# Two more weight tiles in the ring, output-stage norms on DVE, a regrouped scatter and a reordered end of the last expert layer

## The chip, the cores and the metric

The kernel runs on one core of a Trainium2 chip. The metric is the device time of one execution in microseconds (us); several executions are taken and their median counts. One profiled execution gives the trace. Engines: PE is TensorE (PEld its weight loads), DVE is VectorE, ACT is ScalarE, POOL is GpSimd, SP is SyncE, which here only issues DMAs.

## What the kernel computes

Two layers over 512 latent tokens of width 1024 and, in layer 0, 256 context tokens that share the weights. Everything is float32.

```python
def layer(x, l):                      # the latent stream; context likewise in layer 0
    sh1, sc1, g1, sh2, sc2, g2 = split(silu(c) @ w_mod[l] + b_mod[l], 6)
    z = (layer_norm(x) * (1 + sc1) + sh1) @ w_in[l]
    y = concat(multiscale_pool(z), spatial_gating(z), attention(z)) @ w_out[l]
    x = layer_norm(ALPHA * x + g1 * y, ln1_g[l], ln1_b[l])
    h = layer_norm(x) * (1 + sc2) + sh2
    aff = softmax(h @ w_router[l])              # 16 experts
    gate, idx = top_k(aff.T, 64)                # each expert takes 64 of the 512 tokens
    hid = silu(h[idx] @ w1) * (h[idx] @ w3)     # w1, w3, w2: 1024 x 1024 for each expert
    m = zeros.at[idx].add((hid @ w2) * gate)
    return layer_norm(ALPHA * x + g2 * m, ln2_g[l], ln2_b[l])
```

## The kernel before

`Net` runs `mixer`, `output` and the experts for each of the two layers. SP's order is written by hand everywhere: each weight tile is loaded when its place in a ring of tiles comes free, in the order of the code. The other engines are ordered by a planner in the first half of the output stage and by hand (the code's order) from the second half on and in the experts.

**Output stage (`output`).** `cats` holds the mixer's result, turned, as a high and a low part; the weights `w_out` are split likewise (`whi`, `wlo`, `ready`), and a product of a 128-token tile with 512 columns is three matmuls for each of eight k (`mm3`). Half 0 is done for all latent tiles, then half 1. In half 1 the tiles move through a pipeline over m, one tile a step: `product`, `residual` (times g1, plus ALPHA times the residual, statistics), `variance`, `norm1` (first normalisation), `gained` and `shifted` (times ln1's gain, plus its bias), `variance2`, `norm2` (second normalisation), `table` (rows stored to HBM for the gathers), `turn` (transposes), `score` (router product) and `logit`. The last latent tile is "urgent" and is worked in halves. GpSimd computes 1/sigma as a power in `rstd`; `shift` makes -m * r for ACT's normalisation. `router` then finds each expert's 64 tokens by eight rounds of max and match on DVE, and `mod_group` and `gates2` make g2 for the experts. In layer 0 two context tiles are worked in the same stage after the latent ones.

**Experts of layer 1 (`experts_last`).** `weight_stream` hands out tiles of 1 MB (four for a 1024 x 1024 matrix) in a fixed round: ring1 3, cat 4, ring2 5, ring 4, ring3 1, 17 in all. cat is the mixer's result, ring2 the output stage's weights, ring3 the place of its remaining buffers; the tiles of ring hold w_mod's groups 10 and 11 until `mod_group` has used them. `fetch` gathers an expert's 64 rows on GpSimd's queue, four experts ahead, into xg; `inputs` turns them and applies scale (DVE) and shift (GpSimd). Expert e is then worked as first (w1), second of e - 1 (w2), third (w3). The results of two experts make a pair: `second` writes them to two half tiles, which are split into `yhi` (ACT) and `ylo` (DVE, GpSimd), and `scatter` adds them to the token rows by a product with one-hot columns (`picks`), 8 products and 8 DVE additions in a pair. Pairs are (0,1) to (14,15). For the last pair, `base` puts the rows into eight PSUM banks by a product with the identity, the pair is added there, and `total` normalises each tile: statistics, ACT normalisation, gain (GpSimd and DVE), bias (DVE), store. `affine` spreads ln2's gain and bias over the partitions, at expert 13.

Layer 0's experts (`experts`, not changed) work both streams with gathers and scatter-adds over HBM.

## Time and profile before

| what | us |
|---|---|
| median of 3 runs | 1815.21 (1815.08 to 1815.95) |
| the profiled execution | 1820.27 |
| its span, first to last instruction | 1818.5 |
| PE busy | 1624.8 (89%) |
| DVE / ACT / POOL busy | 649.1 / 399.5 / 371.8 |
| DMA | 527.19 MB, 290 GB/s in the mean |

In the order of the trace: the mixer of layer 0 until about 320, its output stage until about 430, its experts until about 980, the mixer of layer 1 until about 1215, its output stage and router until 1315, its experts and the end until 1818.5. Matmuls are pipelined, so that a busy PE is not PE at its peak. A row in order of time reads: start in us, duration in us, engine, line of the kernel, operation, output<-input by the tiles' names, partitions x elements, and in brackets the idle time before it with what ended it. One float32 matmul of the code leaves two records, one of the split products one.

### The profile page before, as it was taken

To read this page: it belongs to the slowest core of one execution; us is meant where nothing else is said; L and a number is where in the kernel's file an instruction comes from. 1 tells how busy PE (TensorE), PEld (TensorE's weight loads), DVE (VectorE), ACT (ScalarE), POOL (GpSimd) and SP (SyncE) were. 2 spreads that over 40 slices of the span, in tenths; PEclk is the share of its full clock that TensorE was granted. 3 is DMA by queue.
4 is the path that set the end of the run, shared out by engine and by line. 5 is a ranking of instruction groups with operands and counts; after the bars stand their busy time and mean duration, and the time that the engine had idled before them with its cause. 6 is when DMAs were issued, how large, how long until landed. Compare 5 with 4: busy or idle time off the path is not lost. (4 is left out here: it accounts for less than half of the span.)

```text
span 1818.5 us, 26146 instructions
## 1 busy us (share of the span) xinstructions
PE 1624.8 (89%) x10859; PEld 849.2 (47%) x10859; DVE 649.1 (36%) x1360; ACT 399.5 (22%) x742; POOL 371.8 (20%) x352
## 2 busy tenths in 40 slices
PE   6988997996999999999996888998699988987994
PEld 3766874752444444344432666776233332332231
DVE  4443663683111111111115855666512221222124
ACT  3333664243000000000002534562300000000001
POOL 2422211142212212112112432212101010100003
PEclk9999999997999999999997898999699999999998
DMA  9441029368999999999997271134899999999992
GB/s 330 149 156 47 1 77 339 134 226 324 362 401 397 396 400 398 395 400 392 401 393 241 79 258 56 54 136 173 319 380 408 409 408 409 409 409 409 409 409 99
DMA packets 160606, 527.19 MB, mean 290 GB/s; under 512 B 10548, under 2 KB 13620, under 8 KB 160232
## 3 DMA queue, kind: packets, MB, share of 16 engines
q1 hardware_dynamic: 147172, 489.47, 69.5%
q0 software_dynamic: 10720, 27.46, 5.1%
q10 hardware_dynamic: 2596, 8.59, 1.2%
q8 instruction: 86, 1.41, 0.3%
q14 instruction: 32, 0.26, 0.0%
HBM read 506.61 MB, written 18.87 MB: 289 GB/s over the span
## 5 line engine op out<-in xcount | busy, mean ns | idle before, releaser
L1325 PE MATMUL h<-ring,xT 128*64 128x512 f32 x1448 | 326.3, 599 | 15.4 <-DMA ring<-in_w 11.5
L1325 PEld LDWEIGHTS h<-ring,xT 128*64 128x64 f32 x1448 | 100.0, 137 | 217.4 <-issue 187.8
L1325 PE MATMUL y<-ring,gpart 128*64 128x512 f32 x760 | 172.8, 597 | 8.6 <-DMA ring<-in_w 7.6
L216 PE MATMUL s<-whi,cat 128*128 128x512 f32 x352 | 147.3, 420 | 10.3 <-ACT whi L884 6.1
L217 PE MATMUL s<-wlo,cat 128*128 128x512 f32 x352 | 145.4, 413 | 8.6 <-DVE wlo L212 7.5
L218 PE MATMUL s<-whi,cat 128*128 128x512 f32 x352 | 144.3, 410 | 2.3 <-DVE cat L430 2.3
L1325 PE MATMUL h<-cat,xT 128*64 128x512 f32 x600 | 137.5, 602 | 6.4 <-DMA cat<-in_w 4.3
L1577 POOL DMA_INDIRECT acc<-y,rows x32 | 51.0, 1594 | 396.7 <-DVE y L1576 396.5
L1325 PEld LDWEIGHTS y<-ring,gpart 128*64 128x64 f32 x760 | 51.9, 137 | 119.8 <-issue 108.9
L1344 ACT ACTIVATE hT<-tr 128x64 f32<-128x64 f32 x34 | 7.3, 225 | 423.0 <-DVE hT L1346 421.3
L1405 DVE SCALAR_TENSOR_TENSOR half<-y,gates,g 64x512 f32<-64x512 f32 x32 | 24.0, 750 | 183.3 <-PE y L1325 182.9
L216 PEld LDWEIGHTS s<-whi,cat 128*128 128x128 f32 x352 | 69.2, 198 | 31.7 <-ACT whi L884 8.7
L217 PEld LDWEIGHTS s<-wlo,cat 128*128 128x128 f32 x352 | 69.2, 197 | 29.0 <-DVE wlo L212 10.8
L1325 PEld LDWEIGHTS h<-cat,xT 128*64 128x64 f32 x600 | 41.2, 138 | 88.1 <-issue 75.5
L1344 ACT ACTIVATE gpart<-tr 128x256 f32<-128x256 f32 x32 | 12.3, 384 | 313.3 <-DVE gpart L1346 313.2
L754 DVE TENSOR_REDUCE am<-s 128x1 f32<-128x768 f32 (+1 forms) x68 | 65.9, 970 | 37.1 <-PE s L751 36.9
L218 PEld LDWEIGHTS s<-whi,cat 128*128 128x128 f32 x352 | 69.1, 196 | 18.9 <-DVE cat L430 3.5
L1325 PE MATMUL c<-ring,xT 128*32 128x256 f32 x1344 | 77.6, 380 | 0.0
L751 PE MATMUL s<-kT,qT 128*128 128x256 f32 (+1 forms) x288 | 71.4, 370 | 5.9 <-ACT zq L766 5.5
L766 ACT ACTIVATE zq<-s,anm 128x768 f32<-128x768 f32 (+1 forms) x80 | 65.1, 816 | 27.2 <-DVE anm L756 26.2
L152 PE MATMUL bk<-ring,cc 128*32 128x512 f32 x384 | 53.5, 676 | 19.1 <-DMA ring<-in_w_mod 18.5
L800 PE MATMUL po<-y,Z 128*64 128x128 f32 x832 | 67.1, 285 | 2.1 <-DVE zt L817 2.1
(350 smaller groups left out, 2297.3 us busy)
## 6 DMA issues: line engine op xcount, KB each, us to landing
ring<-in_w SPq DMA_DIRECT2D x276, 1024.0 KB
cat<-in_w SPq DMA_DIRECT2D x108, 1024.0 KB
ring<-in_w_mod SPq DMA_DIRECT2D x48, 1024.0 KB
ring<-in_w_in SPq DMA_DIRECT2D x12, 1024.0 KB
ring<-in_w_out SPq DMA_DIRECT2D x10, 1024.0 KB
tab<-nn ACTq DMA_DIRECT2D x10, 512.0 KB
acc<-res ACTq DMA_DIRECT2D x6, 512.0 KB
fin<-acc SPq DMA_DIRECT2D x6, 512.0 KB
```

The lines of the kernel that those rows point to most:

```text
L152: nc.tensor.matmul(ps[32 * t:32 * t + 32, :], self.sil[:, k, :], wm[k], start=k < 4, stop=k >= 4)
L216: nc.tensor.matmul(ps, ahi, bhi, start=start, stop=False)
L217: nc.tensor.matmul(ps, ahi, blo, start=False, stop=False)
L218: nc.tensor.matmul(ps, alo, bhi, start=False, stop=stop)
L751: nc.tensor.matmul(sp[:, nk * m + b0:nk * m + b1], qT[t][:, 2 * j + h, :], kT[:, 2 * h + x, k0 + b0:k0 + b1], start=x == 0, stop=x == 1)
L754: nc.vector.tensor_reduce(mx, sp[:, :nk * n].rearrange("p (m k) -> p m k", k=nk), axis=AX.X, op=OP.max)
L766: nc.scalar.activation(pbuf[:, i % 3, nk * m:nk * m + nk], sp[:, nk * m:nk * m + nk], AF.Exp, bias=nm[:, m:m + 1], scale=QK_SCALE, accum_o ...
L800: nc.tensor.matmul(po[t][64 * h:64 * h + 64, 128 * j:128 * j + 128], Z0[:, c0 + c, 128 + 64 * h:192 + 64 * h], pT[:, 128 * c:128 * c + 128 ...
L1325: self.nc.tensor.matmul(outs[s][o:o + cap, :], stat[s][:, k, :], w[k][:, n * t:n * t + n], start=k == 0, stop=k == KC - 1)
L1344: nc.scalar.activation(o[:, r], pv[:, r], AF.Copy)
L1405: nc.vector.scalar_tensor_tensor(ys[j][(r + odd) % 2][p], y[p], gates[p, e:e + 1], g2[odd][p], op0=OP.mult, op1=OP.mult)
L1577: nc.gpsimd.indirect_dma_start(out=self.acc[l, s], out_offset=bass.IndirectOffsetOnAxis(ap=rows[:, e:e + 1], axis=0), in_=y, in_offset=Non ...
```

## The change

1. ring3 of layer 1 has 3 tiles for 1. Room for them: the gathers' xg has 1 buffer for 4, `iota` moves into a tile that stood already, the tiles of ln2's rows go into a ring tile that `take` takes out of the round at expert 6.
2. The gathers run one expert ahead. For expert 0 only its own is issued before its inputs, and scale and shift of expert 0 are done in one operation per 128 columns, half on DVE, half on ACT.
3. Output stage, latent tiles, both layers: `norm1` becomes (x - m) * gain on DVE and `variance2` x * r + bias on DVE, by halves; ACT's first normalisation, GpSimd's gain and DVE's addition go. Context tiles stay.
4. Layer 1: g1's second half is multiplied into the second half of `w_out` in `ready`, and `residual` of half 1 reads PSUM without a product.
5. Layer 1: `mod_group` 10 and 11 move from behind the scores into steps LT and LT + 1 of the pipeline; `gates2` stays.
6. `shift` is a tensor_scalar with r as pointer.
7. Pairs become (0), (1,2) to (13,14), (15); `slots` has a ninth column, filled with -1 where no expert stands. `scatter` comes after the third product. `affine` moves to expert 7. Four bases run within the last w1; within and after the last w3 the pair (13,14) is scattered or added to them. `total`: statistics, (x - m) * gain on DVE out of PSUM, then ACT times r and GpSimd plus bias (the very last half by DVE), store.

```diff
-RING2, RING3 = (2, 5), (7, 1)
+RING2, RING3 = (2, 5), (7, 3)
...
-        self.nc.vector.scalar_tensor_tensor(nb, m, -1.0, r, op0=OP.mult, op1=OP.mult)
+        self.nc.vector.tensor_scalar(nb, m, r, -1.0, op0=OP.mult, op1=OP.mult)
...
             for k in ks:
+                if last and half:
+                    nc.vector.tensor_mul(raw[k], raw[k], g1[0][:, 512:])
...
-            self.iota = self.T(keep, [128, S], "iota")
+            self.iota = self.T(self.small, [128, S], "mpart", bufs=1)
...
+            if last and half:
+                tmp = pss[t]
+            else:
+                tmp = self.T(op, [128, 512], "otmp", bufs=2)
+                nc.vector.tensor_mul(tmp, pss[t], g1[where[t][0]][:, hs])
...
+            if t < LT:
+                for c in halves:
+                    nc.vector.scalar_tensor_tensor(res[t][:, c], res[t][:, c], m, lg[:, c],
+                                                   op0=OP.subtract, op1=OP.mult)
+            else:
+                nc.scalar.activation(res[t], res[t], AF.Identity, bias=self.shift(m, r), scale=r)
...
+                if t < LT:
+                    nc.vector.scalar_tensor_tensor(res[t][:, c], res[t][:, c], mom[t][1], lb[:, c],
+                                                   op0=OP.mult, op1=OP.add)
                 nc.vector.bn_stats(st[:, i], res[t][:, c])
...
-                        for g in range(2):
-                            self.mod_group(l, 10 + g, wm[g])
                         gates2()
...
                     stage(score, m - 3)
+                    if m < LT + 2:
+                        self.mod_group(l, 10 + m - LT, wm[m - LT])
...
-            self.slots = self.T(keep, [128, 2, NE // 2], "slots")
+            self.slots = self.T(keep, [128, 2, NE // 2 + 1], "slots")
+            nc.gpsimd.memset(self.slots, -1.0)
...
+        def take():
+            m = count[0] % len(turns)
+            pool, tag, n = turns[m]
+            turns[:] = turns[m + 1:] + turns[:m]
+            count[0] = 0
+            return self.T(getattr(pool, tag) if pool is self else pool, [128, 2048], tag, bufs=n)
...
+            if e == 0:
+                for b in range(4):
+                    nc.vector.tensor_scalar(o[:, 0, b], pv[:, 0, b], sc2[:, b, 0:1], sh2[:, b, 0:1],
+                                            op0=OP.mult, op1=OP.add)
+                    nc.scalar.activation(o[:, 1, b], pv[:, 1, b], AF.Identity, bias=sh2[:, 4 + b, 0:1],
+                                         scale=sc2[:, 4 + b, 0:1])
+                return
...
+            j, odd = (e + 1) // 2, e % 2
             y = self.P("y")
             self.product(weights("w2", e), {0: y}, {0: hT.pop(e)}, None, odd, between)
+            if e in (0, NE - 1):
+                one = self.T(keep, [128, 512], "half", bufs=2)
+                nc.vector.scalar_tensor_tensor(one, y, gates[:, e:e + 1], g2[odd], op0=OP.mult, op1=OP.mult)
+                ys[j] = [parted(one, nc.vector)] * 2
+                return
...
+        def before_last(j):
+            for i in range(3):
+                yield True
+            for i in range(3):
+                scatter(j, 2 + i // 2, i % 2, "tr")
+                yield True
+                if i < 2:
+                    yield True
+            for i in range(4):
+                add(j, *divmod(i, 2), final[divmod(i, 2)], False, False)
+                if i == 1:
+                    scatter(j, 3, 1, "tr")
+            yield True
...
             for h, c in enumerate(halves):
+                nc.vector.scalar_tensor_tensor(acc[t][:, c], final[t, h], m, norm["g"][:, c],
+                                               op0=OP.subtract, op1=OP.mult)
             yield True
+            for h, c in enumerate(halves):
+                if t == LT - 1 and h == 1:
+                    nc.vector.scalar_tensor_tensor(acc[t][:, c], acc[t][:, c], r, norm["b"][:, c],
+                                                   op0=OP.mult, op1=OP.add)
+                else:
+                    nc.scalar.activation(acc[t][:, c], acc[t][:, c], AF.Copy, scale=r)
+                    nc.gpsimd.tensor_add(acc[t][:, c], acc[t][:, c], norm["b"][:, c])
                 nc.sync.dma_start(self.out[128 * t:128 * t + 128, c], acc[t][:, c])
...
+        fetch(0)
         inputs(0)
+        fetch(1)
+        end = NE - 1
+        for e in range(NE):
+            first(e, (lambda: turn(e - 1)) if e else None, [based()] if e == end else ())
+            if e == NE // 2 - 2:
+                own = self.take()
...
+            if e % 2:
+                picks(e // 2)
             if e:
+                second(e - 1, [affine()] if e == NE // 2 else ())
             inputs(e + 1)
+            fetch(e + 2)
+            late = [before_last(e // 2)] if e == end else []
+            third(e, late)
+            step(late, 100)
+            if e % 2 and e < end:
+                for t in range(LT):
+                    for h in range(2):
+                        scatter(e // 2, t, h)
...
+        second(end)
+        base(2, 0, "h")
+        base(2, 1, "h")
+        for x in range(2):
+            for t in range(2):
+                for h in range(2):
+                    add(j, t, h, final[t, h], False, True, (x,))
...
-        self.xg[e, s] = self.T(self.wk, [128, 1024 // REPS[s]], f"xg{s}", bufs=4 if l == DEPTH - 1 else 3)
+        self.xg[e, s] = self.T(self.wk, [128, 1024 // REPS[s]], f"xg{s}", bufs=1 if l == DEPTH - 1 else 3)
```

## Rows read from the trace of the kernel before

**Rows 1.** The table of stretches, five of layer 1: busy us of each engine, clock, DMA.

```profile
1225.00:1240.00 15.00, 15.00 (x66) 12.06 (x65) 8.43 (x15) 3.44 (x6) 0.00 (x0) 1.00 0.22 87
1262.00:1305.00 43.00, 30.30 (x162) 13.88 (x162) 30.55 (x84) 18.97 (x28) 8.78 (x8) 0.72 1.00 370
1305.00:1325.00 20.00, 11.75 (x47) 5.06 (x48) 2.38 (x13) 0.79 (x4) 5.02 (x5) 0.66 0.52 173
1325.00:1722.00 397.00, 351.94 (x1520) 120.80 (x1518) 87.19 (x150) 22.25 (x42) 33.95 (x32) 0.97 1.03 408
1722.00:1779.00 57.00, 51.81 (x206) 16.74 (x206) 11.91 (x20) 4.68 (x9) 2.33 (x2) 1.00 1.02 405
```

**Rows 2.** Waits of PE by releaser, 440 to 960: us, times, longest.

```profile
PE tr L1334 <- DMA xg<-tab,rows: 2.4, 1, 2.4
```

**Rows 3.** DVE in order of time, both layers: start, us, operation, idle before.

```profile
406.93 2.30 DVE L205 SCALAR_TENSOR_TENSOR lnnb<-lnmv,lnr 128x1 f32<-128x1 f32 x1 [0.51 <-POOL lnr L181]
...
973.36 0.95 DVE L440 CAST whi<-ring 128x512 fp32r<-128x512 f32 x1
...
1252.81 0.69 DVE L934 TENSOR_TENSOR otmp<-s,g 128x512 f32<-128x512 f32 x1 [2.19 <-PE s L218]
...
1269.00 2.31 DVE L205 SCALAR_TENSOR_TENSOR lnnb<-lnmv,lnr 128x1 f32<-128x1 f32 x1 [0.72 <-POOL lnr L181]
...
1271.94 0.69 DVE L935 SCALAR_TENSOR_TENSOR res<-res,otmp 128x512 f32<-128x512 f32 x1
...
1283.22 0.16 DVE L205 SCALAR_TENSOR_TENSOR lnnb<-lnmv,lnr 128x1 f32<-128x1 f32 x1 [0.72 <-POOL lnr L181]
...
1300.80 0.21 DVE L1256 CAST half<-ri 32x128 f32<-32x128 uint32 x1
...
1805.87 7.96 DVE L1453 TENSOR_TENSOR res<-res,norm 128x512 f32<-128x512 f32 x6
```

**Rows 4.** GpSimd in order of time, same columns, both layers.

```profile
406.87 2.33 POOL L960 TENSOR_TENSOR res<-res,lb 128x1024 f32<-128x1024 f32 x1
...
972.91 1.11 POOL L1557 TENSOR_TENSOR hid<-hid,y 128x256 f32<-128x256 f32 x1 [1.49 <-ACT y L1556]
...
1251.98 2.39 POOL L956 TENSOR_TENSOR res<-res,lg 128x1024 f32<-128x1024 f32 x1 [1.55 <-ACT res L949]
...
1268.94 2.34 POOL L956 TENSOR_TENSOR res<-res,lg 128x1024 f32<-128x1024 f32 x1
```

**Rows 5.** PE in order of time, router and first products, both layers.

```profile
360.03 1.61 PE L992 MATMUL bk<-ident,nn 128*128 128x128 f32 x8 [2.63 <-ACT nn L979]
...
1290.47 6.21 PE L152 MATMUL bk<-ring,cc 128*32 128x512 f32 x32
...
1305.51 1.51 PE L1262 MATMUL bk<-ident,half 32*128 32x16 f32 x8 [0.82 <-ACT half L1257]
...
1312.73 1.09 PE L1334 MATMUL tr<-ident,xg 128*128 128x128 f32 x4 [5.71 <-DMA xg<-tab,rows]
...
1315.85 4.63 PE L1325 MATMUL h<-ring,xT 128*64 128x512 f32 x12 [2.03 <-POOL xT L1381]
```

**Rows 6.** The gathers' tile xg, whole run: from issue to landing.

```profile
DMA to landing us min/median/max: 3.5/6.4/7.6
```

**Rows 7.** PE in order of time, the last two products of layer 1.

```profile
1770.71 6.23 PE L1325 MATMUL h<-ring,xT 128*64 128x512 f32 x28
...
1786.07 3.60 PE L1325 MATMUL y<-cat,gpart 128*64 128x512 f32 x16
```

**Rows 8.** Waits of PE, 1315 to 1780, the longest in total.

```profile
PE sc L1419 <- ACT yhi L1410: 16.1, 7, 2.3
```

**Rows 9.** Groups by line and shape, 1779 to the end: busy, mean, idle before.

```profile
L1450 POOL TENSOR_TENSOR res<-res,gain 128x512 f32<-128x512 f32 x6 | 9.3, 1582 | 0.0
L1453 DVE TENSOR_TENSOR res<-res,norm 128x512 f32<-128x512 f32 x8 | 9.2, 1214 | 0.0
...
L1441 DVE BATCH_NORM_STATS2 lnst<-sc 128x6 f32<-128x512 f32 x2 | 1.4, 698 | 1.2 <-PE sc L1439 1.2
```

More of the change, by code (lines that the diff above doesn't have):

```diff
@@ L1384, in stat, with first @@
             return {0: xT[e]}
-        def first(e, middle):
+        def first(e, middle, between=()):
             h1 = self.P("h")
-            self.product(weights("w1", e), {0: h1}, stat(e), middle)
+            self.product(weights("w1", e), {0: h1}, stat(e), middle, between=between)
             hid[e] = self.T(self.small, [128, 512], "gpart", bufs=2)
@@ L1406, in second @@
                                                op0=OP.mult, op1=OP.mult)
[L1407 removed]
+            if not odd:
                 for h in range(2):
[L1409 to L1421 removed]
@@ L1423, in experts_last, with add @@
-        final, norm = {}, {}
-        def base(n, *tags):
-            for m, tag in enumerate(tags, n):
-                t, h = divmod(m, 2)
-                final[t, h] = self.P(tag)
-                nc.tensor.matmul(final[t, h], self.ident, acc[t][:, 512 * h:512 * h + 512], start=True, stop=False)
-                yield True
+                    ys[j][h] = parted(ys[j][h], nc.gpsimd if h else nc.vector)
+        def add(j, t, h, pt, start, stop, xs=(0, 1)):
+            for x in xs:
+                nc.tensor.matmul(pt, oh[j, h][:, 128 * t:128 * t + 128], ys[j][h][x],
+                                 start=start and x == 0, stop=stop and x == 1)
@@ new lines, in scatter, with base, based @@
+        def scatter(j, t, h, tag="sc"):
+            pt = self.P(tag)
+            add(j, t, h, pt, True, True)
+            c = slice(512 * h, 512 * h + 512)
+            nc.vector.tensor_add(acc[t][:, c], acc[t][:, c], pt)
+        final, norm = {}, {}
+        def base(t, h, tag):
+            final[t, h] = self.P(tag)
+            nc.tensor.matmul(final[t, h], self.ident, acc[t][:, 512 * h:512 * h + 512], start=True, stop=False)
+        def based():
+            for i, tag in enumerate(("sc", "sc", "bk", "tr")):
+                base(*divmod(i, 2), tag)
+                yield True
@@ L1436, in total @@
             st = self.T(self.small, [128, 2, 6], "lnst", bufs=4)
             for h in range(2):
-                for x in range(2):
-                    nc.tensor.matmul(final[t, h], oh[j, h][:, 128 * t:128 * t + 128], ys[j][h][x],
-                                     start=False, stop=x == 1)
                 nc.vector.bn_stats(st[:, h], final[t, h])
@@ L1457, in affine @@
         def affine():
-            norm["g"], norm["b"] = self.T(wk, [128, D], "gain"), rows_
+            rows_ = norm["b"]
             banks = []
@@ L1475, in turn @@
             hT[e] = self.hidden(0, hid.pop(e), self.T(self.small, [128, 512], "gpart", bufs=2))
-        rows_ = self.T(wk, [128, D], "norm")
         self.xg = {}
-        for e in range(4):
-            fetch(e)
+        fetch(0)
         inputs(0)
-        for e in range(NE + 1):
-            if e < NE:
-                first(e, (lambda: turn(e - 1)) if e else None)
-            else:
-                turn(e - 1)
-            if e == 1:
-                nc.sync.dma_start(rows_[:2], self.a["ln"][l, 2:4])
-            if e and e % 2 == 0:
-                picks(e // 2 - 1)
-            if e:
-                second(e - 1, {NE - 2: [affine()], NE - 1: [base(0, "sc", "sc", "bk")],
-                               NE: [base(4, "tr", "h", "h")]}.get(e, ()))
-            if e == NE:
-                stages = [total(t) for t in range(LT)]
-                for m in range(LT + 3):
-                    if m == 1:
-                        step([base(7, "y")])
-                    for g in stages[max(0, m - 3):m + 1][::-1]:
-                        next(g)
-            elif e and e % 2 == 0:
-                scatter(e // 2 - 1)
-            inputs(e + 1)
-            fetch(e + 4)
-            if e < NE:
-                third(e, [base(3, "tr")] if e == NE - 1 else ())
@@ new lines, in experts_last @@
+        j = NE // 2
+        turn(end)
+        picks(j)
+        second(end)
[5 more added lines that the diff above has]
+                    add(j, t, h, final[t, h], False, True, (x,))
+        stages = [total(t) for t in range(LT)]
+        next(stages[0])
+        for t in range(2, LT):
+            if t == LT - 1:
+                base(t, 0, "tr")
+                base(t, 1, "y")
+            for h in range(2):
+                add(j, t, h, final[t, h], False, True)
@@ L1508, in gather @@
+        for m in range(1, LT + 1):
+            for g in stages[max(0, m - 1):m + 1][::-1]:
+                next(g)
+                if m > 0 and g is stages[m - 1]:
+                    next(g)
     def gather(self, l, e, s, route):
-        self.xg[e, s] = self.T(self.wk, [128, 1024 // REPS[s]], f"xg{s}", bufs=4 if l == DEPTH - 1 else 3)
+        self.xg[e, s] = self.T(self.wk, [128, 1024 // REPS[s]], f"xg{s}", bufs=1 if l == DEPTH - 1 else 3)
         self.nc.gpsimd.indirect_dma_start(
```

49 lines of the change are left out of this document (12 added, 37 removed).

## The prediction

> **What bounds the kernel now.** I read the page's 40 slices first, then the table of stretches, the waits of PE, and the engines in order of time around the change. The table [rows 1] says that in the experts of layer 1 the DMA engines are full (share 1.03 at 408 GB/s, then 1.02) from 1325 us until the last weight has come at about 1779; so the end of that stream is fixed by where DMA was idle before. The reader is to see one hole: between 1305 and 1325 the share is 0.52. Every tile ahead of the products is loaded by then, and the first comes free only when PE has begun. 0.52 where a full stretch reads 1.03 leaves 20 x (1 - 0.52/1.03) = 9.9 us unused. Behind the stream stands a tail without weights: 1818.5 - 1779 = 39.5 us.
>
> In the experts of layer 0 the bound is PE: from 440 to 960 it waited most for one gather, 2.4 us, and for no weights [rows 2]. There an earlier start of the products moves everything behind it.
>
> **Layer 0, output stage.** `norm1`, `gained` and `variance2` of the latent tiles become four scalar_tensor_tensor on DVE instead of an ACT pass, a GpSimd product and a DVE addition. The price of one is that of the residual's, 0.69 us for 128x512 [rows 3]. DVE's own work of a tile is then the residual 3 x 0.69, two of `norm1` 1.38, four operations of 0.69 in `variance2` 2.76, and small ones about 0.8: 7.0 us, in layer 1 6.3, since the residual loses its product there. Before, it was about 6 plus waits. These waits are the gain: at 1269.00 a 128x1 operation took 2.31 us, because GpSimd's product began at 1268.94 and took 2.34 [rows 3, 4]. The DVE product of PSUM with SBUF at 1252.81 lasted its 0.69 beside GpSimd's product of 1251.98, so only operations on SBUF alone waited. `norm1` also needs only the mean, so GpSimd's power for 1/sigma runs beside it. I replay DVE's order with these prices from the first residual of the second half: the first tile's last normalisation starts about 2 us earlier, and this is the 2.63 us that PE stood before the transposes at 360.03 [rows 5]. PE is nearly full after that, so I take 2.5 us for layer 0; bounds 0.5 (PE's own work decides) and 4. As PE waits for no weights there, it goes through to the end.
>
> **The shift.** `shift` turns from two SBUF inputs into a tensor_scalar with one. In layer 0 it stood for 2.30 us at 406.93 in the middle of the top-k, beside GpSimd's 406.87 [rows 3, 4]. Would the new form wait too? The nearest row with one SBUF input is the cast at 973.36, of 0.95 us beside GpSimd's 972.91 to 974.02 [rows 3, 4]: it waited. So I take nothing for it, and 3 us as the upper bound (2.2 there, about 1 where the layers join).
> The Trainium skill (SBUF — State Buffer, section Who interferes with whom) says that a DVE operation with at most one SBUF input contends with GpSimd only in a two-port mode, and that tensor_scalar is one that can enter it. If a single column does not enter it, that rule gives the 3 us; no row here has this form beside GpSimd.
>
> **Layer 1, from the output stage to the first product.** The eight products that gate the second half of the weights cost DVE 8 x 0.69 = 5.5 us, and four residual products of 0.69 go. DVE is busy 8.43 of the 15 us from 1225 [rows 1], ahead of these weights' splits; the 6.6 idle us hide them. Without that cover PE would wait up to 5.5 us at the start of the second half. Replaying as above, the last tile's shift, at 1283.22 before [rows 3], comes near 1279.3. But one modulation group, half of 6.21 us [rows 5], now lies on PE ahead of that tile's transposes; it takes back 2 to 3, so I keep 1.5. Bounds -1 and 4.
> More certain is the next step: top-k ends on DVE at 1301.0 [rows 3], yet PE reaches its product at 1305.51, because the two modulation groups (from 1290.47) and eight gate products of 1 us lie before it in PE's queue [rows 5]. With the groups moved, the gate products start near 1290 and end before top-k does: 4.3 us. The first expert's inputs skip the GpSimd addition and go by DVE and ACT side by side: 1 of the 3.1 us between 1312.73 and 1315.85 [rows 5]. PE begins 6.8 us earlier, near 1309 on the old time axis.
> The groups' moving also frees four ring tiles earlier; that is worth nothing by itself, since DMA was full from 1262 to 1305 [rows 1], and would be 4 us of stream if it were not.
>
> **Two more ring tiles.** They carry 2.1 MB, 5.1 us at 408 GB/s, so the stream fills until about 1312 instead of 1307. The first tile comes free some 3 us after the first product (TensorE is granted 0.66 in that stretch), and DMA came back about 5 us after that product: now near 1314. Of the 9.9 idle us 2 to 3 stay: 7 gained. Bounds 2 (the added tiles lie over the output stage's last buffers and come free late) and 9.9 (no hole). Their room comes from the gathers' four buffers becoming one. A gather lands 3.5 to 7.6 us after its issue [rows 6] and is issued about one expert before its use, 12.6 MB or 31 us of weights, which hides it; uncovered it would cost PE 6.4 an expert. The tile lent to the norm's rows leaves the ring at the seventh expert; the stream is full then, and loses nothing.
>
> **The tail.** Pairs now begin with expert 0 alone and end with 15 alone, so that 13 and 14 are scattered within the last w3, the affine rows are made at expert 7, and four sums are based within the last w1. Reckon from the last landing L. Before, the last y ended at 1789.67 [rows 7], L + 10.7, though only eight of its 32 records need follow L: PE was behind by the affine rows, the wait for y's halves (16.1 us in seven pairs [rows 8]) and the bases. Now: last w3 tile at L - 10.3 (4.2 MB), its records until L - 8.5, a scatter and the sums of 13 and 14 until L - 5.1, gate product, transposes and copy until L - 4, then 32 records of 0.22 us (28 took 6.23 [rows 7]), 7.0: L + 3.
> Then half, hi and lo, three operations of about 0.7, and the first sums: DVE's statistics start at L + 6.5. DVE has four tiles of 2 x 0.70 and small ones 0.36, and eight products with the gain of about 0.72: 12.8, until L + 19.3 (0.70 is the statistics in [rows 9]). ACT scales beside it. GpSimd adds the bias, 1.2 each by half of its 1024-wide product [rows 4]; the last ones follow DVE, L + 22. Before, GpSimd's products and DVE's additions alternated, 1582 and 1214 ns in the mean [rows 9]; DVE's new products read PSUM and need not wait. From DVE's last addition, which ended at 1805.87 + 7.96 = 1813.83 [rows 3], to the end of the span were 4.7 us. So L + 26.7 against L + 39.5 is 12.8; I take 12, for some waits at the end. Bounds 7 (GpSimd and DVE still alternate in the last six adds, and PE is at half clock in the final sums) and 14.
>
> **Sum.** 2.5 + 7 + 12 = 21.5 us. The profiled execution took 1820.27, its span 1818.5; the median of the runs is 1815.21, 5 below it, and I take the sum off that: 1793.7.
>
> **The rivals.**
> Ring without effect: the added tiles come free when the hole is nearly over. For: they share addresses with what the output stage uses last; against: that use ends near 1290 and these tiles are last in the ring's order. Gain there 2 instead of 7: 1798.7. Chance 0.13.
> Shift free of GpSimd: 3 us more, 1790.7. For: one column, one SBUF input; against: the cast. Chance 0.2.
> Half a tail: PE or GpSimd stays behind, 5 there for 12: 1800.7. Chance 0.09.
> Slower: the single gather buffer. Each gather must wait for the transposes of the expert before. PE is busy 351.94 of 397 us [rows 1], 12.9 experts at 31 us, 27.3 each, 437 for 16; from 1309 to the last y near 1775 (old axis) there are 466, so from 1.8 us of stall an expert PE decides. At 3.1 the change comes to nothing; at 4 it costs 16 x 2.2 = 35: 1829. Against it stands the lead of a whole expert over a landing of 7.6. Chance 0.05, and 0.03 for a stall near 3.
>
> **How the numbers follow.** The forecast holds 0.5: 1793.7, with 1787 to 1799 for it alone, as not all terms fail to one side. The range takes in the free shift and the two weaker gains: 1786 to 1802. A change under 0.2% (3.6 us) is what a measurement of this kernel cannot tell from none. Faster is the sum of forecast, ring, shift and tail, 0.92; within 0.2% 0.03; slower 0.05.
>
> **What would show it.** Right: a DMA share above 0.85 in the 20 us around layer 1's first product; the router's last product on PE as soon as top-k ends; the last y within 5 us of the last landing, and 27 us from that landing to the end; layer 0's experts 2 to 3 us earlier. Wrong: PE waiting for gathers in layer 1, the same hole of 9.9 us, GpSimd additions near 1.6 us in the tail.

## The result, and the profile after

The changed kernel takes 1796.3 us (median, 1793.7 to 1802.6) against 1815.1 for the kernel before in the same series: 0.9901 of it, 95% interval 0.9875 to 0.9927. Forecast were 1793.7 (1786 to 1802) and "faster" at 0.92. So 18.8 us were gained where 21.5 were forecast. The profiled execution took 1802.63 us, its span 1800.8.

Executions of one and the same kernel differ by 8 to 9 us within a series of the changed kernel, and by 18 in one series of the kernel before. Much of it lies before layer 1: in eight profiles with the same code until there, the first product of layer 1's mixer starts anywhere from 992 to 1002 us. From that product to the end three profiles of the changed kernel agree within 0.6 us. So I split this stretch at the same marks in every profile (us between marks, starts of the rows named; "first residual" is DVE's first operation on the results of the output stage's second half):

```
                                                  before   changed (3 profiles)     difference
mixer's first product -> first residual           245.97   243.91 243.66 243.94     -2.1
-> last product of the output stage                21.62    17.67  17.68  17.68     -3.9
-> last cast of the top-k on DVE                   31.99    31.67  31.67  31.66     -0.3
-> the router's last product on PE                  4.71     5.74   5.74   5.73     +1.0
-> transposes of the gathered rows                  7.22     9.60   9.55   9.42     +2.3
-> first product of expert 0                        3.12     1.58   1.58   1.58     -1.5
-> end of the last y                              473.82   464.27 464.30 463.88     -9.7
-> end of the span                                 28.83    24.55  24.60  24.56     -4.3
sum                                               817.28   798.99 798.78 798.45    -18.5
```

The kernel before has one profile of its own in this table. Two later series gained 24.7 and 21.8 us by the medians (below, ref and ref2), more than these 18.5; what layer 0 adds is read further down.

The table of stretches of the changed kernel (times, busy us of PE, PEld, DVE, ACT and POOL, granted clock, DMA share, GB/s), for [rows 1]:

```profile
1264.00:1308.00 44.00, 29.75 (x150) 9.49 (x138) 24.59 (x86) 14.51 (x24) 3.69 (x6) 0.68 1.02 412
...
1304.00:1308.00 4.00, 0.00 (x0) 0.00 (x0) 0.48 (x4) 0.00 (x0) 1.08 (x1) 0.50 1.03 410
1308.00:1312.00 4.00, 1.10 (x6) 0.73 (x6) 0.34 (x1) 0.04 (x1) 0.24 (x1) 0.50 0.09 33
1312.00:1316.00 4.00, 4.00 (x10) 1.23 (x12) 1.03 (x3) 2.74 (x5) 0.74 (x1) 0.50 0.24 66
1316.00:1320.00 4.00, 4.00 (x18) 1.28 (x16) 0.00 (x0) 0.12 (x1) 0.00 (x0) 0.84 0.80 262
...
1770.00:1771.00 1.00, 1.00 (x8) 0.35 (x6) 0.00 (x0) 0.00 (x0) 0.00 (x0) 1.00 0.71 279
1771.00:1772.00 1.00, 1.00 (x8) 0.37 (x6) 0.00 (x0) 0.00 (x0) 0.00 (x0) 1.00 0.44 180
```

The hole is still there. From 1308 to 1320 the shares leave 12 - 4 x (0.09 + 0.24 + 0.80)/1.03 = 7.6 us unused, where 2 to 3 were forecast. What is new stands in the first line: 412 GB/s ahead of the hole, where [rows 1] had 370. In 43 us that is 1.8 MB more, nearly the two added tiles; why the rate rose no run shows. The ring was full at 1308, not at 1312. The stream ends at about 1771 in place of 1779 (read where its share falls off, to some 0.3 us).

PE from the output stage to the first product, for [rows 5]:

```profile
1269.60 3.53 PE L152 MATMUL bk<-ring,cc 128*32 128x512 f32 x16
...
1277.23 1.92 PE L152 MATMUL bk<-ring,cc 128*32 128x512 f32 x16 [0.74 <-DVE rl L1025]
...
1284.73 1.97 PE L1053 MATMUL bk<-gpart,selb 128*64 128x512 f32 x2
...
1298.01 1.97 PE L1055 MATMUL bk<-half,selb 1*64 1x512 f32 x2
1300.80 1.89 PE L1266 MATMUL bk<-ident,half 32*128 32x16 f32 x8 [0.82 <-ACT half L1261]
1310.40 1.09 PE L1349 MATMUL tr<-ident,xg 128*128 128x128 f32 x4 [7.72 <-DMA xg<-tab,rows]
1311.98 7.96 PE L1340 MATMUL h<-ring,xT 128*64 128x512 f32 x24 [0.50 <-DVE xT L1395]
```

The two modulation groups fit into PE's pauses. The eight gate products behind them (first and last shown) take 1.97 us each, where the prediction reckoned with 1, and end at 1299.98. In the kernel before (first and last of the eight, then the granted clock there) they took 1.07 at full clock; in the changed kernel (last line) the clock was at half:

```profile
1296.61 1.07 PE L1049 MATMUL bk<-gpart,selb 128*64 128x512 f32 x2
...
1303.62 1.07 PE L1051 MATMUL bk<-half,selb 1*64 1x512 f32 x2
```

```profile
1297.00:1305.00 8.00, 7.68 (x16) 1.32 (x14) 3.87 (x16) 1.23 (x3) 0.00 (x0) 1.00 1.02 405
```

```profile
1284.00:1300.00 16.00, 15.76 (x18) 2.42 (x18) 10.15 (x42) 3.73 (x5) 0.00 (x0) 0.50 1.02 410
```

DVE had ended the top-k long before, at 1295.27 (last row; the rows ahead of it are for the shift, in both layers):

```profile
406.33 0.21 DVE L205 TENSOR_SCALAR lnnb<-lnmv,lnr 128x1 f32<-128x1 f32 x1 [0.53 <-POOL lnr L181]
...
409.89 1.11 DVE L1259 CAST half<-ri 32x128 f32<-32x128 uint32 x1
...
1276.83 0.21 DVE L205 TENSOR_SCALAR lnnb<-lnmv,lnr 128x1 f32<-128x1 f32 x1 [0.72 <-POOL lnr L181]
...
1295.06 0.21 DVE L1260 CAST half<-ri 32x128 f32<-32x128 uint32 x1
```

GpSimd beside it, in both layers:

```profile
406.27 2.35 POOL L965 TENSOR_TENSOR res<-res,lb 128x1024 f32<-128x1024 f32 x1
408.58 2.34 POOL L961 TENSOR_TENSOR res<-res,lg 128x1024 f32<-128x1024 f32 x1
...
1304.80 1.08 POOL L1576 DMA_INDIRECT xg<-tab,rows  x1 [27.94 <-DVE gates L1287]
```

At 406.33 the shift takes 0.21 us in the middle of a GpSimd addition, where the old form stood 2.30 [rows 3]. The first gather is issued at 1304.80, while weights still stream, and its transposes start 5.6 us later. Behind it PE waits for no other gather; its waits from 1312 to 1772 are mostly for weights, of which this is the largest (us in total, times, longest):

```profile
PE h L1340 <- DMA ring<-in_w: 18.7, 29, 1.2
```

The end: PE's last y, the last operation of DVE and of GpSimd, and GpSimd's group with its mean, for [rows 7] and [rows 9]:

```profile
1769.17 3.65 PE L1340 MATMUL y<-cat,gpart 128*64 128x512 f32 x16 [0.52 <-DVE gpart L1361]
1772.65 3.60 PE L1340 MATMUL y<-ring,gpart 128*64 128x512 f32 x16
```

```profile
1791.34 0.75 DVE L1497 SCALAR_TENSOR_TENSOR res<-res,lnr,ring 128x512 f32<-128x512 f32 x1
```

```profile
1790.19 4.24 POOL L1501 TENSOR_TENSOR res<-res,ring 128x512 f32<-128x512 f32 x3
```

```profile
L1501 POOL TENSOR_TENSOR res<-res,ring 128x512 f32<-128x512 f32 x7 | 9.2, 1338 | 0.9 <-ACT res L1500 0.9
```

With L = 1771 the last y ends at L + 5.3, DVE at L + 21, GpSimd at L + 23.4, the span at L + 30.

### The profile page after: what moved, and what is told of

It reads as the page before. It is cut to its first block, busy times and chain, and to the rows that moved or that the text cites. A ratio compares the mean times of both kernels' runs of the same rounds, so it can differ in the third digit from the quotient of the medians.

```text
span 1800.8 us, 26188 instructions
## 1 busy us (share of the span) xinstructions
PE 1621.4 (90%) x10875; PEld 841.3 (47%) x10875; DVE 643.8 (36%) x1378; ACT 390.7 (22%) x735; POOL 348.2 (19%) x344
## 5 line engine op out<-in xcount | busy, mean ns | idle before, releaser
L1340 PE MATMUL h<-ring,xT 128*64 128x512 f32 x1504 | 343.6, 601 | 21.8 <-DMA ring<-in_w 18.7
L1340 PE MATMUL y<-ring,gpart 128*64 128x512 f32 x720 | 162.5, 596 | 9.3 <-DMA ring<-in_w 8.8
L1340 PE MATMUL h<-cat,xT 128*64 128x512 f32 x544 | 125.7, 604 | 9.9 <-DMA cat<-in_w 7.8
L1340 PEld LDWEIGHTS h<-cat,xT 128*64 128x64 f32 x544 | 37.0, 138 | 85.9 <-issue 69.4
L1340 PE MATMUL y<-cat,gpart 128*64 128x512 f32 x304 | 69.7, 597 | 3.5 <-DMA cat<-in_w 3.0
```

Of the source, the lines that this page charges most:

```text
L1340: self.nc.tensor.matmul(outs[s][o:o + cap, :], stat[s][:, k, :], w[k][:, n * t:n * t + n], start=k == 0, stop=k == KC - 1)
```

## The experiments

Each is judged by the marks above, from its profile, with the medians beside them:

```
                mixer's first     of it, from the  to router's   to expert 0's  to the   sum     median (lowest to highest)
                to output's last  first residual   last product  first product  end
before          267.59            21.62            36.70         10.34          502.65   817.28
ref             261.34            17.68            37.41         11.13          488.90   798.78  1793.1 (1791.6 to 1799.6)
ref2            261.62            17.68            37.39         11.00          488.44   798.45  1797.3 (1790.6 to 1799.8)
e_ring          260.93            17.68            37.36          9.29          494.76   802.34  1796.3 (1793.5 to 1801.7)
e_shift         262.37            17.63            37.26         11.18          488.09   798.90  1796.6 (1793.1 to 1800.4)
e_gates1        259.48            17.69            31.11         12.20          489.03   791.82  1792.2 (1787.7 to 1795.2)
e_gates01       261.49            17.68            31.31         12.13          489.67   794.60  1789.5 (1788.5 to 1790.6)
best            261.61            17.69            31.31         12.14          488.94   794.00  1788.5 (1784.8 to 1793.0)
e_mod11         261.54            17.68            37.39         11.00          487.85   797.78  1792.5 (1789.7 to 1797.8)
e_tail          265.95            21.69            33.58          9.30          494.75   803.58  1803.9 (1801.0 to 1812.1)
e_out0          261.52            17.68            37.40         11.15          489.53   799.60  1796.9 (1794.1 to 1798.3)
e_norm1         261.20            17.25            35.22         12.11          489.41   797.94  1793.6 (1790.7 to 1797.5)
e_ungated       261.76            18.41            38.00          9.74          489.57   799.07  1797.2 (1796.1 to 1800.2)
```

Runs were made in three groups, each on one chip: ref, e_gates1, e_ring, e_shift; then e_tail, e_mod11, e_gates01, e_out0; then ref2, best, e_norm1, e_ungated. The kernel before had medians of 1817.7, 1816.9 and 1819.0 there. In the texts put on record before the runs, "the last product of the mixer" is the output stage's last product.

How far the marks can be trusted is read from runs whose edit lies elsewhere. From the first residual to the output stage's last product nine profiles of the same code give 17.67 to 17.69. Ahead of the first residual profiles of the same code differ by 2.2 us (241.8 in e_gates1 to 244.0 in e_norm1), from expert 0's first product to the end by 1.8 (487.9 to 489.7). Differences below that are not resolved there.

**The changed kernel again (ref).**

> The changed kernel again, unedited, as the measure for the three that run with it on this chip. Its runs so far lie between 1793.7 and 1802.6 us, a wider spread than that of the kernel before (1814.7 to 1816.0), so a difference of a term is read against this run and not against the first ones. Expected: 1794 to 1798.

1793.1, 1 us below the expected span; 0.9861 (0.9839 to 0.9884) of the kernel before on this chip. In the third group 1797.3.

**Two ring tiles less (e_ring).**

```diff
-RING2, RING3 = (2, 5), (7, 3)
+RING2, RING3 = (2, 5), (7, 1)
```

> The changed kernel with one tile in the last ring in place of three, nothing else. Theory of the prediction: the two tiles are 2.1 MB, 5.1 us at 408 GB/s, so the stream stops 5.1 us earlier (at about 1303), DMA's hole is as much longer, and the time is 5 us more. First rival: the tiles come free late and carry nothing: 0 to 1 us more. Second rival: with them DMA is full while the gather is under way, and without them the gather lands faster (3.5 us in place of 5.5 in the changed kernel's trace), which gives 2 us back: 3 us more.

From the first product to the end 5.9 us more: the two tiles carry what the prediction gave them (5.1). But the stretch to the first product is 1.8 shorter. Stretch, gather and transposes of this run, from the table of stretches, GpSimd and PE:

```profile
1292.00:1296.00 4.00, 0.43 (x3) 0.33 (x2) 1.63 (x11) 0.00 (x0) 1.08 (x1) 0.50 0.09 34
```

```profile
1294.56 1.08 POOL L1576 DMA_INDIRECT xg<-tab,rows  x1 [27.91 <-DVE gates L1287]
```

```profile
1298.26 1.09 PE L1349 MATMUL tr<-ident,xg 128*128 128x128 f32 x4 [5.82 <-DMA xg<-tab,rows]
```

DMA is idle when the gather is issued, and it is there after 3.7 us, not 5.6. That is the second rival. The tiles are worth 5.9 - 1.8 = 4.1 us net; the sums of the table give 802.34 - 798.7 = 3.6, the medians 3.3.

**The gates (e_gates1, then both layers: e_gates01).** `gates2` takes the numbers of the tiles that it makes; in layer 1:

```diff
-                        gates2()
+                        gates2((0,))
...
                 step([lat], 100)
+                gates2((1,))
```

> Layer 1: only the first of the two gate tiles (four of eight products) is made before the end of the top-k, the second behind the router's last product, in the time in which PE waits for the gather. Theory, the gate products decide: in the changed kernel they hold PE from 1284.73 to 1299.98 at 1.97 us each while top-k ends on DVE at 1295.2; with four of them PE is free at 1292.6 and the router's last product starts at about 1296.1 instead of 1300.80. The other four (7.9 us) end near 1306, when the gather lands. Then the first product is 4.7 us earlier, the idle stretch of DMA shorter by as much, and the time 4 to 5 us less. Rival, the gather among the weights decides: it is issued earlier into full queues and lands no earlier than about 1309, or the four products stand before its transposes; then 0 to 1.5 us.

> The changed kernel with the second gate tile behind the router in both layers. Layer 1 as in the run with that layer alone: the router's last product 31.1 us after the mixer's last product instead of 37.4, and 5 us less to the end. Layer 0, theory that the gate products decide there too: they end at 412.0 in the changed kernel while the top-k ends at about 411; with four of them left behind the router its last product starts about 1.5 us earlier and the experts of layer 0 with it; 6.5 us less than the changed kernel in all. Rival for layer 0: the context tile's transposes, which wait for DVE and ACT, stand before the gather's in PE's queue and decide: 0 from layer 0.

In layer 1 the router's last product came 6.1 to 6.3 us earlier behind the output stage, the first product 5.0 to 5.2 earlier; one more is lost on the gather, which now lands among weights all the time. PE in the run with both layers:

```profile
1282.62 1.97 PE L1057 MATMUL bk<-half,selb 1*64 1x512 f32 x2
1286.90 1.89 PE L1270 MATMUL bk<-ident,half 32*128 32x16 f32 x8 [2.31 <-ACT half L1265]
1288.72 1.97 PE L1055 MATMUL bk<-gpart,selb 128*64 128x512 f32 x2
...
1297.45 1.08 PE L1353 MATMUL tr<-ident,xg 128*128 128x128 f32 x4 [1.08 <-DMA xg<-tab,rows]
```

PE is idle 2.31 us before the router's product: now top-k decides. So the gate products were the bound in the changed kernel, as the theory said. From the first product to the end nothing changes (488.9 to 489.7), so the 5 us of start go through to the end. The medians of the first group show only 0.9 us of it, the repeat below 8.7: a handful of runs does not resolve such a term. Of e_gates1's sum, 1.9 us lie ahead of the output stage's last product, where nothing was edited. In layer 0, from the first residual of the second half to the first expert product, 83.8 in place of 85.5: 1.8 us, but 0.8 of them lie ahead of the gate products. The 1.0 behind the last product is of the size expected; TensorE's clock moves this stretch by more (see e_out0), so for layer 0 the theory is not shown.

**One modulation group back before the gates (e_mod11).**

```diff
+                        self.mod_group(l, 11, wm[1])
                         gates2()
...
-                    if m < LT + 2:
+                    if m < LT + 1:
```

> The changed kernel with the second modulation group back in front of the gate products (the first stays beside the scores). In the kernel before both groups (6.21 us) stood there and the gate products behind them took 1.07 us each; in the changed kernel PE has pauses there and they take 1.97. Theory, what PE did before sets the granted clock: the group takes 3.5 us at half clock from 1284.7 on, the eight gate products about 1.07 each behind it, and the router's last product starts about 4 us earlier: 33.5 us after the last product of the mixer instead of 37.4. Rival, the clock stays at 0.50 behind one group: the group and the products together last 19 us, the router's product comes 3 us later, 40.5.

Neither: 37.39, as without the edit. PE:

```profile
1277.52 3.64 PE L152 MATMUL bk<-ring,cc 128*32 128x512 f32 x16
1281.09 1.97 PE L1053 MATMUL bk<-gpart,selb 128*64 128x512 f32 x2
1282.99 1.08 PE L1055 MATMUL bk<-half,selb 1*64 1x512 f32 x2
...
1287.47 1.96 PE L1055 MATMUL bk<-half,selb 1*64 1x512 f32 x2
```

and its clock:

```profile
1281.00:1283.00 2.00, 2.00 (x7) 0.30 (x3) 1.97 (x9) 0.60 (x1) 0.00 (x0) 0.50 1.02 408
1283.00:1287.00 4.00, 4.00 (x9) 0.75 (x8) 3.90 (x17) 0.60 (x1) 0.00 (x0) 0.93 1.03 410
1287.00:1293.00 6.00, 6.00 (x7) 0.86 (x6) 0.98 (x5) 0.00 (x0) 0.00 (x0) 0.50 1.03 410
```

The clock did rise to full speed behind the group, but it was taken back at 1287 while the gate products went on. Gates and group together take as long as the gates alone at half clock. What kept it up for eight products in the kernel before is left open; both groups back in front were not tried.

**The end alone (e_tail).** The kernel before with `experts_last`, `take`, the slots and the single gather buffer of the changed one.

> The kernel before with only the experts of layer 1 changed (regrouped pairs, bases, affine rows at expert 7, gathers one ahead, first inputs on DVE and ACT, the norms of the end). The ring, the output stage, the shift, the gates and the modulation groups stay as before. Theory: from the last landing to the end 39.2 becomes 29.9 as in the changed kernel, since nothing else in the change touches that stretch; the first product comes 1.5 us earlier; so 9.5 to 11 us less than before in all, and from layer 1's first product to the end 493 us instead of 502.7. Prediction on record: 12 from the last landing. Rival: part of the 9.3 us came from the earlier stream, and the regrouping alone gives 5.

From the first product to the end 494.75 for 502.65: 7.9 us, 1.8 less than the theory's 493 stands for. The rival of 5 is out. The inputs take 1.6 in place of 3.1, as in the changed kernel. In all it is 13.7 us faster by the marks, 13.0 by the medians, more than the 9.5 to 11 expected: 4.8 of it lie before the router's product, where nothing was edited. 1.7 of these come ahead of the first residual, 3.1 behind the output stage, where both modulation groups took 3.64 us for 6.21 (granted clock from 1290 to 1297: 1.00 for 0.59). Whether chance or a side effect, one profile each leaves open; by it, the column of the kernel before may be up to 4.8 us too slow in the first table. In its output stage, which is the old one, DVE and PE show the stall that the change was to remove:

```profile
1259.43 2.31 DVE L205 SCALAR_TENSOR_TENSOR lnnb<-lnmv,lnr 128x1 f32<-128x1 f32 x1 [0.65 <-POOL lnr L181]
```

```profile
1263.07 1.82 PE L992 MATMUL bk<-ident,nn 128*128 128x128 f32 x8 [2.63 <-ACT nn L979]
...
1289.29 3.64 PE L152 MATMUL bk<-ring,cc 128*32 128x512 f32 x32
```

**The old shift (e_shift).**

```diff
-        self.nc.vector.tensor_scalar(nb, m, r, -1.0, op0=OP.mult, op1=OP.mult)
+        self.nc.vector.scalar_tensor_tensor(nb, m, -1.0, r, op0=OP.mult, op1=OP.mult)
```

> The changed kernel with the old form of the shift (scalar_tensor_tensor with two SBUF inputs). Theory now: the one-column tensor_scalar was 0.21 us beside GpSimd in layer 0 (406.33) and where the layers join, the old form 2.3 and 1.2, but in layer 0 the gate products on PE end later than the top-k anyway and take that back; where the layers join an addition waits in its place (1.62 for 0.68). So 1 to 2 us more, from the join. Rival, the prediction's choice: no difference, 0. Rival with the full sum of the stalls: 3 us more.

The stall is back, DVE and GpSimd in layer 0:

```profile
398.33 2.29 DVE L205 SCALAR_TENSOR_TENSOR lnnb<-lnmv,lnr 128x1 f32<-128x1 f32 x1 [0.52 <-POOL lnr L181]
```

```profile
398.26 2.33 POOL L965 TENSOR_TENSOR res<-res,lb 128x1024 f32<-128x1024 f32 x1
```

and costs nothing in layer 1's output stage (17.63 for 17.68), nothing that can be resolved in layer 0 (85.0 from the first residual of the second half to the first product, for 85.5) and 0.1 in the sum against ref. Ahead of layer 1's first residual it reads 0.8 more than the highest of the unedited profiles. The median is 3.5 higher, but the runs of the two overlap. By the marks it is nearest to the prediction's 0; up to 1 us cannot be excluded.

**Old norms in layer 1, and in layer 0 (e_norm1, e_out0).** `norm1`, `gained`, `shifted` and `variance2` take the lines of the kernel before for that layer.

> The changed kernel with the old norms (ACT pass, GpSimd product, DVE addition) in layer 1's output stage alone; gated weights, shift and layer 0 as changed. Measured from the first to the last product of layer 1's mixer: 267.6 us in the kernel before, 261.3 to 261.6 in the changed one. Theory now: the norms are most of these 6 us, since the old ones make the first tile's transposes wait on PE (2.63 us) and the products behind them; 265 to 266, and 4 to 5 us more in all. Prediction on record: 1.5 us for the whole output stage of layer 1. Rival: the gated weights are most of it, and it reads 262 to 263.

> The changed kernel with the old norms (ACT pass, GpSimd product, DVE addition) in layer 0's output stage alone; the shift stays the new form and layer 1 as changed. Measured from the first residual of layer 0's second half to the first expert product there: 86.1 us in the kernel before, 85.5 in the changed one. Theory now: PE's own order and the gate products decide, so the norms are worth 0 to 0.8 us, and it reads 85.5 to 86.3. Prediction on record: 2.5 us, so 88.

My theory fell: with the old norms in layer 1 it reads 261.20, not 265, and behind the output stage the top-k ends 1.7 us earlier. So beside the new shift the new norms gain nothing in layer 1: the first expert product comes 1.6 us earlier without them, counted from the first residual. In the sum that is 0.5 to 1.0 us, which is not resolved. The shift in its new form stands beside GpSimd's products without waiting, and the transposes have no wait either, DVE, GpSimd and PE of this run:

```profile
1253.83 0.21 DVE L205 TENSOR_SCALAR lnnb<-lnmv,lnr 128x1 f32<-128x1 f32 x1 [0.72 <-POOL lnr L181]
```

```profile
1253.77 2.36 POOL L970 TENSOR_TENSOR res<-res,lg 128x1024 f32<-128x1024 f32 x1
```

```profile
1250.02 1.03 PE L1009 MATMUL bk<-ident,nn 128*128 128x128 f32 x8
```

In layer 0, from the first residual of the second half, the fourth tile's residual comes at 24.1 us where norms and shift are old (before, e_tail), at 21.3 with the new shift alone (e_out0), at 21.3 with the new norms alone (e_shift) and at 21.4 with both. Either edit brings the 2.7 us. The two later marks depend on TensorE's clock as well: in the 12 us from 45 us on it stayed full in some profiles and fell to half for a time in others, with the same code. From the first residual of the second half (us):

```
layer 0 as in              profiles                   clock, 45 to 57   last product   first expert product
kernel before              before                     1.00              57.9           86.1
kernel before              e_tail                     0.86              59.3           90.0
changed kernel             e_norm1, e_gates1          1.00              55.2           83.4
changed kernel             after, ref, ref2, e_mod11  0.86              56.5           85.5 to 85.6
changed kernel             e_ring, e_ungated          0.86              56.6           87.5
changed, old norms         e_out0                     0.86              57.9           86.9
changed, old shift         e_shift                    0.86              56.0           85.0
changed, gate tile behind  e_gates01, best            0.86              55.8           83.8
```

The rows of these 12 us for before, e_norm1, e_tail and the changed kernel:

```profile
388.44:400.44 12.00, 9.53 (x41) 6.60 (x40) 10.47 (x28) 4.35 (x7) 3.70 (x4) 1.00 0.57 219
382.58:394.58 12.00, 10.95 (x54) 7.05 (x54) 10.84 (x33) 4.46 (x7) 3.60 (x3) 1.00 0.38 130
387.14:399.14 12.00, 9.52 (x34) 6.64 (x34) 10.21 (x28) 4.35 (x7) 3.52 (x3) 0.86 0.56 218
389.84:401.84 12.00, 10.98 (x42) 7.89 (x46) 10.16 (x31) 4.04 (x6) 3.59 (x3) 0.86 0.32 124
```

With the clock full in both, the changed layer 0 is 2.7 us earlier at the last product and still 2.7 earlier at the first expert product; with the clock fallen in both, 2.7 to 2.8 and 2.5 to 4.5. Behind these 12 us the clock fell at different gate products, which parts 85.5 from 87.5. What makes it fall in one execution and not in another is left open. Read against the four profiles with its clock, e_out0 is 1.3 later at both marks: beside the new shift the norms are worth 1.3 us there, on the last tile, somewhat over the 0 to 0.8 that I expected.

**Ungated weights (e_ungated).**

```diff
-                if last and half:
-                    nc.vector.tensor_mul(raw[k], raw[k], g1[0][:, 512:])
...
-            if last and half:
-                tmp = pss[t]
-            else:
-                tmp = self.T(op, [128, 512], "otmp", bufs=2)
-                nc.vector.tensor_mul(tmp, pss[t], g1[where[t][0]][:, hs])
+            tmp = self.T(op, [128, 512], "otmp", bufs=2)
+            nc.vector.tensor_mul(tmp, pss[t], g1[where[t][0]][:, hs])
```

> The changed kernel without the gated weights: the residuals of layer 1's second half multiply by the gate again, on DVE, as in layer 0; the norms stay new. Theory: the four products of 0.69 us lie on the chain of DVE that ends the output stage, and two or three of them come back, 1.5 to 2.5 us later to the last shift and to the first expert product. Prediction on record: the eight products on the weights are hidden, and the four that go were part of 1.5 us. Rival: DVE waits for PE there anyway, 0 to 0.5.

The output stage took 0.7 us more (18.41), the top-k ended 1.3 us later behind it, but the gather took 4.2 us in place of 5.6 and the first product came no later: 0.1 to 0.6 in the sum, nothing in the medians. The rival holds for the end.

**The version to keep (ref2, best).** The changed kernel with the second gate tile behind the router in both layers, beside the changed kernel.

> The changed kernel again, unedited, beside the version with the second gate tile behind the router, on one chip. Expected 1793 to 1797, and from the last product of layer 1's mixer to the end 537.4 us, as in its two earlier profiles.

> The changed kernel with the second gate tile behind the router in both layers, again, beside the unedited changed kernel. Theory: 5 us less in layer 1 and 1 in layer 0, so 5 to 6 us less than the changed kernel on this chip, 1788 to 1791. Rival: the gain of the one profile is given back elsewhere, and the medians differ by less than 2 us.

1788.5 against 1797.3, 0.9837 (0.9816 to 0.9858) and 0.9878 (0.9858 to 0.9898) of the kernel before; the marks give 4.5 us in layer 1 and 1.8 in layer 0, so 2.4 of the 8.7 between the medians, where 5 to 6 were expected, have no mark. It is the fastest version measured. The old norms in layer 1 (e_norm1) were not tried in it. The hole in the stream shrank to one slice, 4 x (1 - 0.42/1.03) = 2.4 us:

```profile
1304.00:1308.00 4.00, 4.00 (x18) 1.28 (x16) 0.34 (x1) 1.97 (x3) 0.00 (x0) 0.76 0.42 96
```

## Why the prediction was right in the sum, step by step

The terms were 2.5 + 7 + 12; measured are about 2.7, 8 and 9.7. Yet none of the signs of being right came as written: the DMA share in the 20 us around the first product was 0.64 for 0.85, the router's last product stood 5.7 us behind the top-k, the last y ended at L + 5.3 and the span at L + 29.8, and layer 0's experts began 0.8 us later in the profiled pair. That the ring's term came near is luck; the other two held by their mechanisms, each with a step that failed.

**Layer 0, 2.5.** The replay of DVE was right: the fourth tile comes 2.7 us earlier. At equal clock this goes through to the first expert product, as forecast (86.1 to 83.4). In the profiled pair it is hidden: TensorE's clock fell to half for a time in the changed kernel's profile and not in the other, which left 1.3 us at the last product and 0.6 at the first expert product, and the changed kernel came to this stage 1.4 us late. The step that failed is whose gain it is: with the new shift the old norms reach the fourth tile as early, and the norms add 1.3, at the last tile.

**The shift, 0.** The sum's value holds about; the reason for it was wrong. The cast at 973.36 [rows 3] was the wrong nearest row: the new form takes 0.21 us beside GpSimd everywhere.
The Trainium skill (SBUF — State Buffer, section Who interferes with whom) has tensor_scalar contend only in a two-port mode; the rows at 406.33 and in e_norm1 agree with that for a single column, with 0.21 us inside GpSimd's 2.35 and 2.36.
But the rival's 3 us did not come. In layer 0 a cast then waited in its place (409.89, 1.11 us beside GpSimd's 408.58), and the gate products ended after the top-k anyway. Where it paid was the output stage, for which I had not priced it: with the new shift the old norms do no harm in layer 1 (e_norm1), with the new norms the old shift does little (e_shift). Two cures of one stall; one alone would do, and I had given the gain to the norms. The fourth tile of layer 0 shows all four cases; in layer 1 both old forms were not run with the gated weights, which are worth 0.7 us of the 3.9 beside the new ones (e_ungated).

**Layer 1's start, 6.8.** Measured from the mixer's first product, 4.5: output stage 3.9 + 0.3 where I kept 1.5, since the modulation group on PE took nothing back; gates -1.0 where I had +4.3; inputs 1.5 for 1; a loss of 2.3 at the gather that I had not thought of; and 2.1 ahead of the first residual, of which e_tail has 1.7 without an edit there, so not the change's. "The gate products end before top-k does" is the step that failed: they were priced at the 1 us of the kernel before, where they stood behind 6 us of modulation products; without these in front they ran at half clock, 1.97 us. That the missing groups alone lowered the clock is likely and not shown (e_mod11). e_gates1 shows the loss: 5 us.

**Two ring tiles, 7.** The tiles' load was priced right (5.1, measured 5.9), the hole wrongly. 7.6 of its 9.9 us stayed, because the ring filled at 412 GB/s instead of 370, so it was full 4 us before 1312, and PE's start came later than forecast. "DMA was full from 1262 to 1305" read the share of 1.00 in [rows 1] and not the 370 GB/s beside it, 38 below a full stretch. What counts is not the hole: from PE's first product the stream's end is fixed by the tiles already loaded. The stream ended 8 us earlier: 5.3 by the tiles (from the first product to its end about 459.1 in ref, 464.4 in e_ring and in e_tail), 4.5 by the earlier start, less 0.6 lost before layer 1 and 1.2 from the first product on, apart from the tiles (463.2 before). Right size, other shares, and the gather gives 1.8 of the tiles' gain back. The rival of tiles without effect is out, and so is that of the single gather buffer: PE waits for one gather, the first.

**The tail, 12.** From L = 1779 to the end 39.5, now 29.8: 9.7. The mechanism is as forecast: DVE took 12.7 us from its first statistics (12.8 forecast), GpSimd 1.34 us an addition (1.2 forecast; its products of the kernel before took 1.58), and ended 2.3 us after DVE. Mis-sized were the last y, at L + 5.3 for L + 3, as the sums of 13 and 14 reach until 1768, and the 6.4 us from the last addition to the end, for 4.7. e_tail gives 7.9 us for the same lines alone: some 9.1 from L on, less the 1.2 lost ahead of L.

## What to carry to other kernels

Price an instruction at the clock it will meet in its new place, not at that of its old one: the gate products took 1.07 us behind the modulation groups and 1.97 without them. Where two edits remove the same stall, price them alone and together, or the gain is given to the wrong one. Where the whole time varies more than the terms, split it at marks that every profile has: one stretch repeated within 0.1 us where the medians of one kernel differed by 4. But see first what each stretch does in profiles of the same code, and compare profiles with the same granted clock: one profile against one hid 2 us of layer 0's gain here.

## What was not expected of the hardware

The transposes of the first expert's gather start 3.7 us after its issue where the weights' stream has stopped (before, e_ring, e_tail), 5.4 to 6.6 us where weights still stream (changed, e_gates1): more prefetched weights delay the small transfer that everything waits for. With the same code TensorE's clock stayed full in some profiles and fell to half in others (layer 0: 1.00 or 0.86 in the same 12 us), which moved the first expert product between 83.4 and 87.5 us. It fell from full to half at 1287 in e_mod11 while it was busy without a pause with products of 1 and 128 rows in fp32. A stall beside GpSimd that the shift no longer takes went to another operation: to a cast in layer 0 (1.11 us), and in the join of the layers to the addition in line 386 (1.62 us for 0.68).
